# A hybrid S5 and differential-attention layer: the 1/rms chain of a head's outputs on GpSimd, the second map's factor as a tensor-scalar operation

## The chip, the cores and the metric

The kernel runs as one program on one core of a Trainium2 chip. The metric is the device time of one execution in microseconds (us); a kernel's time is the median of its runs. The engines are written as in the profile: PE (TensorE, with PEld for its weight loads), DVE (VectorE), ACT (ScalarE), POOL (GpSimd) and SP (SyncE, which here only issues DMAs).

## The reference, cut to what matters

The layer projects 1040 tokens (16 meta tokens and 1024 of input), runs an S5 mixer and a differential attention side by side, merges both by gates, and ends in a feed-forward stage. The change touches the attention, which has 8 heads with two softmax maps each:

```python
    s = jnp.einsum('bqhtd,bkhtd->bhtqk', qb, k, ...) * scale + bias[None, :, None]
    p = jax.nn.softmax(s, axis=-1)
    w = p[:, :, 0] - lam32 * p[:, :, 1]
    return jnp.einsum('bhqk,bkhe->bqhe', w.astype(v.dtype), v)
...
    xf = xf * lax.rsqrt(jnp.mean(xf * xf, axis=-1, keepdims=True) + EPS)   # _rmsnorm of a head's 128 outputs
...
    o = _rmsnorm(o, attn_subln[layer]) * (1.0 - lam_init)
    y_attn = o.reshape(bsz, L, ATTN_WIDTH) @ w_attn_out[layer]
```

## The kernel before

**Tiles and steps.** A head has 8 query tiles of 128 rows. Two tiles, a and b, make a pair, and the attention is a loop over 32 pairs, four steps to a head. What a step issues, and in which order, is written out by hand in a string (STEPS): each entry is an action and how many steps behind the newest pair it runs. The order of that string is the order in which each engine gets its instructions, since every engine works through its own instructions in order.

**What a step does.** PE makes the scores of a tile (L1163, L1164; six pieces, C10, C11, C12 for the second map and C00, C01, C02 for the first) into four PSUM buffers called S. DVE adds the bias, takes the minimum and writes the piece to the tile E0 or E1 (L1175, actions c10 to c02); each of E0 and E1 has two buffers, so a tile's E1 can be written only when POOL has read the E1 of two tiles earlier. ACT takes the exponential with its sum Z (L1181). DVE computes 1/Z and the second map's factor (L1187 and L1188, action coef; the factor is lambda times Z0/Z1). POOL scales E1 by the factor, adds E0 and E1 reversed into w, and copies 16 columns (L1195, L1197, L1198, action comb). PE transposes w (L1204, action T), ACT and DVE split the result into a high and a low part (L1214, L1218, actions hi and lo), and PE multiplies it with the values (L1239, action PV). Between these, PE does a gated linear unit of the S5 branch (L92 to L94, action GLU); its last product is one POOL instruction a step (L1374, action post2). POOL also splits a weight (L174) about once a head and scales a head's outputs (L1297, action mulq) twice a head.

**The chain.** ACT sums the squares of a tile's outputs (L1259). When a head's 8 tiles are done, the generator o_norm turns the 8 sums into 1/rms by an integer first guess and three Newton steps, on tiles of 128x8 (ss, ory, ora). It yields after each operation, and the actions n3a, n2b, n3b, n1a, n1b, n0a, n2a, n0b of a step each run it to its next yield. So a head's chain takes eight yields in one step and four in the next. These two of a head's four steps are called its chain steps below, and the other two its plain steps:

```python
STEPS = (... "sqb:4 ... mulq:1 ... n3a:3 ... combb:2 ... n2b:4 PV2y:3 post:2 exp0a:1 lo1a:2 n3b:4 n1a:2 n1b:1 post2:2 "
         "coefa:1 bcC:3 ... n0a:2 n2a:2 ... n0b:0 c00b:1 T1b:2 c01b:1 exp1b:1 hi1b:2 comba:1 GLUb:1 ")
for s_ in "ab":
    for n in range(4):
        FREE[f"n{n}{s_}"] = lambda: next(norm[0], None)
```

The result is read one step later by a transpose on PE (action bcT) and then, by way of DMAs, by L1297. Head 6 runs its chain in the string after the loop (TAIL, action n), and head 7 after that, when POOL has no work.

Of the kernel before, what the change touches and what calls it, by code (L numbers as in the profile page):

```python
# [11 lines left out]
I32 = mybir.dt.int32  # L12
AF = mybir.ActivationFunctionType
ALU = mybir.AluOpType
# [10 lines left out]
EPS = 1e-6  # L25
NT = S // 128
# [25 lines left out]
def tile_hybrid_encoder(ctx, tc, A, out, dbg=None, stop=None):  # L52
    nc = tc.nc
# [28 lines left out]
    V = nc.vector  # L82

    def mul(o, a, b):
        V.tensor_tensor(out=o, in0=a, in1=b, op=ALU.mult)
# [617 lines left out]
    nlam = cst.tile([128, 1], F32, tag="nlam", name="nlam")  # L703
# [114 lines left out]
    def warm(n):  # L818
        ps = pst([128, 512], "sm", "warm")
        for _ in range(n):  # L820
# [6 lines left out]
                           op1=ALU.add, accum_out=ms[:NM, 0:1])  # L827
# [302 lines left out]
    def ptl(pool, tag, shape, dt=F32, bufs=1):  # L1130
        return pool.tile(shape, dt, tag=tag, name=tag, bufs=bufs)
# [52 lines left out]
    def w_coef(i):  # L1184
        t = IT[i]
        rz = HT[i // NT]["rz"][:, i % NT]
        V.reciprocal(rz, t["Z"])  # L1187
        V.scalar_tensor_tensor(out=t["cf"][:, 0:1], in0=rz[:, 1:2], scalar=nlam, in1=t["Z"][:, 0:1],  # L1188
                               op0=ALU.mult, op1=ALU.mult)

    def w_comb(i):

# [65 lines left out]
        tp = PO["t", i // 2][:, i % 2]  # L1258
        nc.scalar.activation(tp, tp, AF.Square, scale=hd["rz"][:, qt, 0:1], accum_out=hd["ss"][:, qt:qt + 1])  # L1259

    def o_norm(h, a, b):

        hd = HT[h]
        ss, rz = hd["ss"][:, a:b], hd["rz"][:, a:b, 0]
        if a == 0:
            hd["y"] = ptl(osp, "ory", [128, NT], F32, 3)
        y, v = hd["y"][:, a:b], ptl(osp, "ora", [128, NT])[:, a:b]
        V.tensor_scalar(out=ss, in0=ss, scalar1=1.0 / 128, scalar2=EPS, op0=ALU.mult, op1=ALU.add)
        yield
        V.tensor_scalar(out=y.bitcast(I32), in0=ss.bitcast(I32), scalar1=-0.5, scalar2=float(0x5F3759DF),  # L1270
                        op0=ALU.mult, op1=ALU.add)
        yield
        for _ in range(3):
            mul(v, y, y)
            yield
            V.scalar_tensor_tensor(out=v, in0=v, scalar=-0.5, in1=ss, op0=ALU.mult, op1=ALU.mult)
            yield
            V.scalar_tensor_tensor(out=y, in0=v, scalar=1.5, in1=y, op0=ALU.add, op1=ALU.mult)
            yield
        mul(y, y, rz)  # L1280
        yield

    def o_bcT(h):
# [188 lines left out]
    norm = [iter(())]  # L1472
# [22 lines left out]
    for x in range(2):  # L1495
        s_ = "ab"[x]
        for m in range(2):
            ACTS[f"exp{m}{s_}"] = lambda p, m=m, x=x: ex_map(2 * p + x, m)
            for c in range(3):
                ACTS[f"C{m}{c}{s_}"] = lambda p, m=m, c=c, x=x: sc_mm(2 * p + x, m, c)  # L1500
                ACTS[f"c{m}{c}{s_}"] = lambda p, m=m, c=c, x=x: sc_tt(2 * p + x, m, c)
        for n, f in (("T", w_T), ("hi", w_hi), ("lo", w_lo)):
            for g in range(3):
                ACTS[f"{n}{g}{s_}"] = lambda p, f=f, g=g, x=x: f(2 * p + x, g)
        for n, f in (("coef", w_coef), ("comb", w_comb), ("sq", o_sq)):
            ACTS[n + s_] = lambda p, f=f, x=x: f(2 * p + x)
# [36 lines left out]
    def c_fill():  # L1543

        for us in (0,), (1,):
            for n in range(KD - 1):
                for c in range(2):
                    c_mm(us[0], c, 0, n, n + 1)
                    yield

    cf = c_fill()
# [4 lines left out]
    def run(steps):  # L1556
        for n in steps.split():
            n, _, p = n.partition("@")
            ACTS[n](int(p)) if p else FREE[n]()
# [12 lines left out]
    for j in range(3, NP + 1):  # L1572
# [8 lines left out]
        def at_(k, d):  # L1581

            h, q = divmod(j - d - k, 4)
            return h if q == 0 and 0 <= h < H else None

        h = at_(1, LC)
        if h is not None:
            load_head(h + 1)
        h = at_(3, LC)
        if h is not None:  # L1590
            load_q(h + 1, 1)
        h = at_(3, LP - 4)
        if h is not None:
            load_v(h + 1)
        h = at_(3, LS + 7)
        if h is not None and h < H - 3:
            o_st(h)
        h = at_(3, LS + 2)
# [4 lines left out]
        h = at_(3, LS)  # L1603
        if h is not None:
            norm[0] = o_norm(h, 0, NT)
    def tail_o():
# [3 lines left out]
        for a, n in ((0, 2), (2, 2), (4, 1)):  # L1610
# [4 lines left out]
                 "s0": lambda: o_split(0, 0, 2), "s1": lambda: o_split(0, 2, 2), "s2": lambda: o_split(0, 4, 1),  # L1615
                 "w0": lambda: w_next(U_A[0], 0), "w1": lambda: w_next(U_A[0], 1), "f": fill_c(1)})
    run(TAIL)
    norm[0] = o_norm(7, 0, NT)
    assert not (mulq or fill or wq or any(GQ))
    o_fa(6, 2)  # L1620
    o_fa(6, 3)
# [503 lines left out]
```

## Time and profile before

| | |
|---|---|
| median of 3 runs | 1904.03 us (1900.61 to 1904.47) |
| the profiled execution, its own time | 1903.11 us |
| its span, first to last instruction | 1900.9 us |
| PE busy | 1827.6 us (96%) |
| DVE busy | 1268.6 us (67%) |
| ACT, POOL busy | 867.9 us (46%), 871.6 us (46%) |
| mean granted TensorE clock | 0.989 |

The span is what the trace covers; 2.2 us of the execution's own time lie around it. The shares are means over the whole program. The loop over the pairs takes the time from about 690 to 1080 us, and there the busy shares are 95% for PE, 90% for DVE, 72% for ACT and 73% for POOL.

### The profile page before, as it was taken

Reading aid. Unit: us, or ns where it says so; the run is one execution under the profiler, and the core shown is the slowest. Engines: PE = TensorE matmul, PEld = TensorE weight load, DVE = VectorE, ACT = ScalarE, POOL = GpSimd, SP = SyncE. Lnnn points to the kernel's source line nnn. Section 1 sums busy time; section 2 is a strip of 40 time slices with the busy share of each in tenths; the row PEclk is TensorE's granted clock in tenths of the full one; section 3 lists DMA queues with packets and bytes.
Section 4 is the critical chain, followed back from the end, with each engine's and each line's share of the span. In section 5 each row is a group of like instructions: output and inputs, shape, how many; then the busy total and the mean of one; then the engine's idle time right before and its main releaser. Section 6 shows DMA issues by size and latency. Waiting matters only on the chain. (4 is left out here: it accounts for less than half of the span.)

```text
span 1900.9 us, 31037 instructions
## 1 busy us (share of the span) xinstructions
PE 1827.6 (96%) x11306; PEld 1642.2 (86%) x11306; DVE 1268.6 (67%) x2601; ACT 867.9 (46%) x1597; POOL 871.6 (46%) x803
## 2 busy tenths in 40 slices
PE   8998999899999989999999899999999999999999
PEld 7997888889999889999999888998788887888887
DVE  6699997763544688989999864369554545654543
ACT  4324343233433367777767632234555554433332
POOL 3068999643332177777767500005765652400000
PEclk8999999999999999999999999999999999999999
DMA  7423323337678565454554346431644448986563
GB/s 218 121 76 86 99 89 109 99 103 235 234 245 290 199 172 148 128 155 140 154 145 143 108 161 219 133 117 56 214 146 157 148 156 304 345 282 202 183 210 116
DMA packets 230535, 315.89 MB, mean 166 GB/s; under 512 B 39560, under 2 KB 140472, under 8 KB 230344
## 3 DMA queue, kind: packets, MB, share of 16 engines
q1 hardware_dynamic: 209952, 283.14, 47.1%
q10 hardware_dynamic: 20432, 30.78, 4.4%
q8 instruction: 89, 1.46, 0.3%
q14 instruction: 62, 0.51, 0.1%
HBM read 212.28 MB, written 99.48 MB: 164 GB/s over the span
## 5 line engine op out<-in xcount | busy, mean ns | idle before, releaser
L89 DVE TENSOR_TENSOR fp<-fr,fp 128x1024 fp32r<-128x1024 f32 x112 | 141.1, 1306 | 128.0 <-ACT fp L88 127.4
L92 PE MATMUL ps<-wh,hnh 128*128 128x256 f32 x768 | 221.3, 288 | 4.7 <-DVE qraw L969 3.5
L93 PE MATMUL ps<-wh,hnl 128*128 128x256 f32 x768 | 219.1, 285 | 4.6 <-DVE hnl L89 4.6
L94 PE MATMUL ps<-wl,hnh 128*128 128x256 f32 x768 | 218.8, 285 | 0.0
L88 ACT CAST fp<-fr 128x1024 fp32r<-128x1024 f32 x112 | 110.4, 1050 | 180.8 <-PE pf L94 159.2
L94 PE MATMUL pf<-fp 128*128 128x512 f32 x448 | 174.5, 390 | 1.3 <-DVE fp L89 1.3
L92 PE MATMUL pf<-fp 128*128 128x512 f32 x448 | 174.5, 390 | 0.5 <-ACT fp L88 0.4
L93 PE MATMUL pf<-fp 128*128 128x512 f32 x448 | 174.3, 389 | 0.0
L1181 ACT ACTIVATE E<-E,st 128x1040 f32<-128x1040 f32 x128 | 149.4, 1167 | 47.4 <-DVE st L1175 37.7
L1175 DVE CUSTOM_DVE_ANT_0 E<-S,Tb,st 128x344 f32<-128x344 f32 x256 | 146.7, 574 | 27.1 <-PE S L1164 5.7
L1197 POOL TENSOR_TENSOR w<-E,E 128x1040 f32<-128x1040 f32 x64 | 155.4, 2427 | 5.3
L92 PEld LDWEIGHTS ps<-wh,hnh 128*128 128x128 f32 x768 | 147.7, 192 | 6.9 <-DVE qraw L969 4.1
L93 PEld LDWEIGHTS ps<-wh,hnl 128*128 128x128 f32 x768 | 147.8, 192 | 4.9 <-DVE hnl L89 4.8
L94 PEld LDWEIGHTS ps<-wl,hnh 128*128 128x128 f32 x768 | 148.0, 193 | 0.0
L1163 PE MATMUL S<-K,Q 128*128 128x344 f32 (+1 forms) x384 | 134.5, 351 | 3.1 <-issue 3.0
L92 PE MATMUL ps<-hnh,wh 128*128 128x512 f32 (+2 forms) x352 | 133.6, 380 | 0.0
L93 PE MATMUL ps<-hnh,wl 128*128 128x512 f32 (+2 forms) x352 | 132.3, 376 | 1.3 <-POOL wl L174 1.0
L94 PE MATMUL ps<-hnl,wh 128*128 128x512 f32 (+2 forms) x352 | 131.4, 373 | 0.0
L89 DVE TENSOR_TENSOR swl<-w1r,swh 128x512 fp32r<-128x512 f32 x70 | 79.6, 1167 | 70.4 <-ACT swh L88 70.3
L1214 ACT CAST W<-wt 128x384 fp32r<-128x384 f32 x192 | 89.3, 481 | 79.3 <-PE wt L1204 71.6
L1164 PE MATMUL S<-K,Q 128*128 128x344 f32 (+1 forms) x384 | 123.5, 323 | 0.0
L1195 POOL TENSOR_SCALAR E<-E,st 128x1040 f32<-128x1040 f32 x64 | 74.4, 1163 | 97.1 <-DVE st L1188 55.3
(428 smaller groups left out, 5328.4 us busy)
## 6 DMA issues: line engine op xcount, KB each, us to landing
fr<-ad SPq DMA_DIRECT2D x56, 512.0 KB
ad<-r SPq DMA_DIRECT2D x91, 256.0 KB
raw<-in_w_in_dram SPq DMA_DIRECT2D x44, 512.0 KB
w<-in_w_ff_dram SPq DMA_DIRECT2D x32, 512.0 KB
wd<-w SPq DMA_DIRECT2D x32, 512.0 KB
Q<-qd SPq DMA_DIRECT2D x128, 128.0 KB
fr<-wd SPq DMA_DIRECT2D x32, 512.0 KB
w1r<-in_w_ff_dram SPq DMA_DIRECT2D x28, 512.0 KB
```

The source lines that it names most:

```text
L88: nc.scalar.copy(hi, src)
L89: (eng or nc.vector).tensor_tensor(out=lo, in0=src, in1=_f(hi), op=ALU.subtract)
L92: nc.tensor.matmul(o, l[0], r[0], start=start, stop=False, **kw)
L93: nc.tensor.matmul(o, l[1], r[0], start=False, stop=False, **kw)
L94: nc.tensor.matmul(o, l[0], r[1], start=False, stop=stop, **kw)
L1163: nc.tensor.matmul(ps[:, 0:n], qa[:, qs], k, start=True, stop=False)
L1164: nc.tensor.matmul(ps[:, 0:n], qb[:, qs], k, start=False, stop=True)
L1175: V.tensor_tensor_reduce(out=t["E", m][:, c0:c0 + n], in0=t.pop(("S", m, c))[:, 0:n], in1=HT[h]["Tb"][:, b0:b0 + n], scale=1.0, scalar=mn ...
L1181: nc.scalar.activation(t["E", m], t["E", m], AF.Exp, bias=t["mn"][:, m:m + 1], scale=-1.0, accum_out=t["Z"][:, m:m + 1])
L1195: nc.gpsimd.tensor_scalar(out=E1, in0=E1, scalar1=t["cf"][:, 0:1], scalar2=0.0, op0=ALU.mult, op1=ALU.add)
L1197: nc.gpsimd.tensor_tensor(out=w[:, 112:], in0=_rev(E0), in1=_rev(E1), op=ALU.add)
L1214: nc.scalar.copy(WT[p, g][:, :, 0, x], IT[i]["tp", g])
```

## The change

o_norm gets an engine and takes GpSimd where none is given, so the chains of heads 0 to 6 move from DVE to POOL. GpSimd gets no scalar_tensor_tensor here: the -0.5 becomes one extra operation ahead of the Newton steps, and the +1.5 one extra in each of the three. A chain of 12 instructions becomes one of 16. The number of yields stays at 12, so each operation stands at the same place in STEPS. Head 7 is given VectorE by name and runs the new 16 operations there. Beside this, w_coef computes the factor by a tensor_scalar with two per-row scalars, where it was a scalar_tensor_tensor.

```diff
-        V.scalar_tensor_tensor(out=t["cf"][:, 0:1], in0=rz[:, 1:2], scalar=nlam, in1=t["Z"][:, 0:1],
-                               op0=ALU.mult, op1=ALU.mult)
+        V.tensor_scalar(out=t["cf"][:, 0:1], in0=rz[:, 1:2], scalar1=nlam, scalar2=t["Z"][:, 0:1],
+                        op0=ALU.mult, op1=ALU.mult)
...
-    def o_norm(h, a, b):
+    def o_norm(h, a, b, eng=None):
+        G = eng or nc.gpsimd
...
-        V.tensor_scalar(out=ss, in0=ss, scalar1=1.0 / 128, scalar2=EPS, op0=ALU.mult, op1=ALU.add)
-        yield
-        V.tensor_scalar(out=y.bitcast(I32), in0=ss.bitcast(I32), scalar1=-0.5, scalar2=float(0x5F3759DF),
+        G.tensor_scalar(out=ss, in0=ss, scalar1=1.0 / 128, scalar2=EPS, op0=ALU.mult, op1=ALU.add)
+        yield
+        G.tensor_scalar(out=y.bitcast(I32), in0=ss.bitcast(I32), scalar1=-0.5, scalar2=float(0x5F3759DF),
                         op0=ALU.mult, op1=ALU.add)
+        G.tensor_scalar(out=ss, in0=ss, scalar1=-0.5, scalar2=None, op0=ALU.mult)
         yield
         for _ in range(3):
-            mul(v, y, y)
+            G.tensor_tensor(out=v, in0=y, in1=y, op=ALU.mult)
             yield
-            V.scalar_tensor_tensor(out=v, in0=v, scalar=-0.5, in1=ss, op0=ALU.mult, op1=ALU.mult)
+            G.tensor_tensor(out=v, in0=v, in1=ss, op=ALU.mult)
             yield
-            V.scalar_tensor_tensor(out=y, in0=v, scalar=1.5, in1=y, op0=ALU.add, op1=ALU.mult)
+            G.tensor_scalar(out=v, in0=v, scalar1=1.5, scalar2=None, op0=ALU.add)
+            G.tensor_tensor(out=y, in0=v, in1=y, op=ALU.mult)
             yield
-        mul(y, y, rz)
+        G.tensor_tensor(out=y, in0=y, in1=rz, op=ALU.mult)
         yield
...
-    norm[0] = o_norm(7, 0, NT)
+    norm[0] = o_norm(7, 0, NT, V)
```

On POOL, in the first chain step of head 0, the order before holds the comb of tile b, post2 and the comb of tile a, one behind the other (E is a map, w the combined tile, sg the gated product):

```order
L1195 TENSOR_SCALAR E_8466<-E_8466,st 128x1040
L1197 TENSOR_TENSOR w_7406<-E_8517,E_8466 128x1040
L1198 COPY w_7406<-w_7406 128x16
L1374 TENSOR_TENSOR sg<-ggt,sg 128x256
L1195 TENSOR_SCALAR E_8573<-E_8573,st 128x1040
L1197 TENSOR_TENSOR w_7405<-E_8594,E_8573 128x1040
```

The same place after the change, from the copy of tile b's comb on (ss, ory and ora are the chain's tiles):

```order
L1198 COPY w_7406<-w_7406 128x16
L1271 TENSOR_SCALAR ory<-ss 128x8
L1273 TENSOR_SCALAR ss<-ss 128x8
L1276 TENSOR_TENSOR ora<-ory 128x8
L1278 TENSOR_TENSOR ora<-ora,ss 128x8
L1280 TENSOR_SCALAR ora<-ora 128x8
L1281 TENSOR_TENSOR ory<-ora,ory 128x8
L1377 TENSOR_TENSOR sg<-ggt,sg 128x256
L1276 TENSOR_TENSOR ora<-ory 128x8
L1278 TENSOR_TENSOR ora<-ora,ss 128x8
L1280 TENSOR_SCALAR ora<-ora 128x8
L1281 TENSOR_TENSOR ory<-ora,ory 128x8
```

Ten instructions of the chain now stand between the comb of tile b and the comb of tile a: six ahead of post2 (L1377 now) and four behind it.

On DVE, at the same place, the order before holds the chain among the low parts, the scores and the factor:

```order
L1218 TENSOR_TENSOR W<-wt,W 128x3x128
L1270 TENSOR_SCALAR ory<-ss 128x8
L1368 SCALAR_TENSOR_TENSOR sg<-sg,f 128x256
L1218 TENSOR_TENSOR W<-wt,W 128x3x128
L85 TENSOR_TENSOR ora<-ory 128x8
L1276 SCALAR_TENSOR_TENSOR ora<-ora,ss 128x8
L1278 SCALAR_TENSOR_TENSOR ory<-ora,ory 128x8
L1187 RECIPROCAL rz<-st 128x2
L1188 SCALAR_TENSOR_TENSOR st<-rz,nlam,st 128x1
L1175 ISA E_8666,st<-S,Tb_7842 128x352
```

The same place after the change:

```order
L1218 TENSOR_TENSOR W<-wt,W 128x3x128
L1371 SCALAR_TENSOR_TENSOR sg<-sg,f 128x256
L1218 TENSOR_TENSOR W<-wt,W 128x3x128
L1187 RECIPROCAL rz<-st 128x2
L1188 TENSOR_SCALAR st<-rz,nlam,st 128x1
L1175 ISA E_8668,st<-S,Tb_7842 128x352
```

The chain's rows are gone from DVE, and the factor (L1188) is a tensor-scalar operation; the order of the rest is the same.

## Rows read from the trace of the kernel before

**Rows 1.** Waits of PE in the attention loop: total us, times, longest us

```profile
PE wt L1204 <- DVE W L1218: 13.6, 8, 2.1
PE ot L1253 <- DVE W L1218: 4.8, 7, 1.0
```

**Rows 2.** Chain-step pairs, heads 0 to 5: us, busy (count) PE PEld DVE ACT POOL

```profile
751.75:778.54 26.79, 25.04 (x195) 24.14 (x193) 24.99 (x82) 18.05 (x43) 16.55 (x14) 1.00 0.50 140
...
sum 167.41, PE 153.23 PEld 147.78 DVE 156.29 ACT 109.28 POOL 108.63; mean PE 25.54 PEld 24.63 DVE 26.05 ACT 18.21 POOL 18.10
```

**Rows 3.** The same for the six plain-step pairs that follow them

```profile
778.54:802.01 23.47, 23.47 (x187) 23.24 (x186) 20.47 (x70) 18.38 (x41) 18.99 (x16) 1.00 0.48 135
...
sum 140.74, PE 140.74 PEld 139.42 DVE 123.07 ACT 110.36 POOL 117.22; mean PE 23.46 PEld 23.24 DVE 20.51 ACT 18.39 POOL 19.54
```

**Rows 4.** Timeline in head 2's first chain step: start us, us, engine, line

```profile
861.45 2.41 POOL L1197 TENSOR_TENSOR w<-E,E 128x1040 f32<-128x1040 f32 x1
...
861.76 2.12 DVE L85 TENSOR_TENSOR ora<-ory 128x8 f32<-128x8 f32 x1
...
864.00 0.55 DVE L1218 TENSOR_TENSOR W<-wt,W 128x384 fp32r<-128x384 f32 x1
...
864.61 0.55 PE L1204 MATMUL wt<-idn,w 128*128 128x128 f32 x3 [1.47 <-DVE W L1218]
```

**Rows 5.** Instructions on tile ora, all heads: ns min/median/max, first and last start

```profile
L85 DVE TENSOR_TENSOR ora<-ory x24: 156/450/2311, 756.5 to 1097.8; 128x8 f32<-128x8 f32 x24
...
L1278 DVE SCALAR_TENSOR_TENSOR ory<-ora,ory x24: 150/168/931, 757.2 to 1098.2; 128x8 f32<-128x8 f32 x24
```

**Rows 6.** Line 1270, the chain's first guess, columns as above

```profile
L1270 DVE TENSOR_SCALAR ory<-ss x8: 172/766/785, 755.1 to 1095.8; 128x8 int32<-128x8 int32 x8
```

**Rows 7.** Line 1188, the factor, columns as above

```profile
L1188 DVE SCALAR_TENSOR_TENSOR st<-rz,nlam,st x64: 219/219/1100, 662.9 to 1073.9; 128x1 f32<-128x1 f32 x64
```

**Rows 8.** POOL's timeline in the S5 set-up, instructions of 128x8

```profile
283.73 1.19 POOL L356 TENSOR_TENSOR TC<-TC,e 128x8 f32<-128x8 f32 x1
284.88 0.20 POOL L357 TENSOR_TENSOR tt<-TS,e 128x8 f32<-128x8 f32 x1
285.16 0.21 POOL L358 TENSOR_TENSOR TC<-TC,tt 128x8 f32<-128x8 f32 x1
285.33 0.20 POOL L356 TENSOR_TENSOR TS<-TC,e 128x8 f32<-128x8 f32 x1
```

**Rows 9.** Groups by shape on POOL, dearest of 128x8: busy us, mean ns

```profile
L356 POOL TENSOR_TENSOR TS<-TC,e 128x8 f32<-128x8 f32 x7 | 3.6, 520 | 0.0
```

**Rows 10.** Line 1197, the comb's sum on POOL: ns min/median/max

```profile
L1197 POOL TENSOR_TENSOR w<-E,E x64: 2397/2428/2523, 667.4 to 1075.5; 128x1040 f32<-128x1040 f32 x64
```

**Rows 11.** Timeline of a plain step (head 1 to 2): POOL's comb, first users

```profile
846.38 0.74 POOL L1374 TENSOR_TENSOR sg<-ggt,sg 128x256 f32<-128x256 f32 x1
...
847.63 1.14 POOL L1195 TENSOR_SCALAR E<-E,st 128x1040 f32<-128x1040 f32 x1 [0.50 <-DVE st L1188]
...
848.85 2.44 POOL L1197 TENSOR_TENSOR w<-E,E 128x1040 f32<-128x1040 f32 x1
...
...
851.50 1.30 POOL L1297 TENSOR_TENSOR osb<-osb,fb 128x512 f32<-128x512 f32 x1
...
852.73 0.52 DVE L1175 CUSTOM_DVE_ANT_0 E<-S,Tb 128x352 f32<-128x352 f32 x1
...
854.18 0.41 PE L1163 MATMUL S<-K,Q 128*128 128x344 f32 x1
...
855.05 0.49 PE L1204 MATMUL wt<-idn,w 128*128 128x128 f32 x3
```

**Rows 12.** POOL's timeline around the start of head 1's first chain step

```profile
801.80 1.30 POOL L1297 TENSOR_TENSOR osb<-osb,fb 128x512 f32<-128x512 f32 x1
```

**Rows 13.** PE's timeline behind the loop, where head 6's chain runs

```profile
1070.42 0.55 PE L1204 MATMUL wt<-idn,w 128*128 128x128 f32 x3 [1.80 <-DVE W L1218]
...
1078.65 0.55 PE L1204 MATMUL wt<-idn,w 128*128 128x128 f32 x3 [1.03 <-DVE W L1218]
```

## The prediction

> **What bounds the kernel now.** I read the page first: PE is busy 96% of the span, so only work that PE waits for can move the time, and the first question is where PE waits. In the attention loop the list of waits gives it two that count, both for the low parts that DVE makes of the transposed w: 13.6 and 4.8 us [rows 1]. DVE, not PE, is late there. Next I cut the loop into pairs of steps at DVE's factor of a tile b and set the pairs with a chain beside those without. The plain pairs are PE's alone: PE is busy for all of the 140.74 us of six of them, 23.46 us each [rows 3]. The chain pairs take 167.41 us for six, PE is idle for 14.2 of these (167.41 - 153.23), and DVE is busy 156.29 us where the plain pairs have 123.07 [rows 2, 3]. So the chain costs PE time, though PE does almost none of it.
>
> The timeline shows how. In head 2 the chain's square of 128x8 on DVE begins at 861.76 and takes 2.12 us; POOL's sum of two 128x1040 tiles runs from 861.45 to 863.86, and the little DVE instruction ends with it, at 863.88. The low part behind it starts at 864.00, and PE has then stood 1.47 us [rows 4]. The same square takes 156 ns at its fastest and 2311 at its slowest, the chain's product 150 and 931 [rows 5]; the first guess has a median of 766 ns against 172 when POOL has nothing to do (the last of the eight, head 7's) [rows 6]. These DVE instructions wait for POOL's running one. The factor does too, at times: 219 ns as a rule, 1100 at most [rows 7].
>
> **What is removed.** Six heads (0 to 5) have chain pairs between plain pairs. The pairs can't be compared as they stand, because DVE's lateness shifts the cut: a chain pair holds 195 matmuls and a plain pair 187 [rows 2, 3]. A pair with the mean of 191 at the plain pairs' pace takes 23.46 x 191 / 187 = 23.96 us. Twelve such pairs take 287.5 us where they now take 167.41 + 140.74 = 308.15. So **20.6 us** is all that the loop can give back, 3.4 us a head. It fits the idle 14.2 us and the longer busy time of PE where it stops and starts again. Behind the loop, in head 6's chain, PE waits 1.80 and 1.03 us for low parts held the same way [rows 13]; I count **2.0** of these 2.8, since comb and outputs of the last tiles are short of other work to hide behind.
>
> **What is added on POOL.** Sixteen instructions of 128x8 a head. Unhindered ones take 0.20 us in the set-up, and one that reads its forerunner's result starts 0.28 us after it (284.88 to 285.16), one that doesn't 0.17 us (285.16 to 285.33) [rows 8]. Each of the chain needs the one before, so I take 0.28 each, 4.5 us a head. The trace has no chain of tensor-scalar operations of this size on POOL; the ends are 0.17, and 0.60 from the dearest group's mean of 520 ns with the 0.08 between [rows 9]. I stay near the low end because POOL's comb sum, 64 times in this loop, always takes between 2397 and 2523 ns [rows 10]: POOL isn't held there by DVE, and after the change DVE has still fewer instructions that could.
>
> POOL is busy 18.10 us of a chain pair and 19.54 of a plain one [rows 2, 3]. With 4.5 more it has 22.6 of some 24 us: nearly full, but with room to recover in the plain pair. What counts is who waits for it inside the chain step. One instruction stands ahead of comb b, where POOL waits for the factor anyhow. Ten stand between comb b and comb a, 2.8 us. In a plain step POOL goes from comb b's copy straight to post2 at 846.38, then stands 0.50 us and starts comb a at 847.63 [rows 11]; in a chain step comb a then starts 2.5 us later (2.8 with the small gaps, less the 0.5, and POOL's start behind the last small one), its sum ends at about 853.8 instead of 851.29. Two users follow. PE's transposes of that w begin at 855.05, 3.5 us after POOL is through with the comb (its next instruction starts at 851.50), so they stay covered. DVE writes the next E1 at 852.73, 1.4 us behind the sum that must have read the old one [rows 11]: **DVE now waits 1.1 us there**, with its factor and all later scores behind it. PE's matmul at 854.18 needs the S buffer that this DVE instruction frees at 853.25; its 0.93 us of slack [rows 11] leave 0.2 us of PE time.
>
> In heads 1, 3 and 5 it is worse: the scaling of outputs runs on POOL up to 803.10, 1.1 us into the step that begins at 802.01 [rows 12], where in the other heads the scaling is done before the step (it ends at 852.8, [rows 11]). There comb a is about 1.2 us later again, DVE waits 2.3 us, PE 1.3 or 1.4. The second chain step has five small instructions, four of them between the combs, 1.1 us, and starts late; its comb a delays DVE by 0.7 us, inside the 0.93. So POOL takes back 3 x 0.2 + 3 x 1.3 = **4.5 us**.
>
> **The factor.** A tensor-scalar operation with one tensor input: the nearest rows are 219 ns for the form before and 172 for a tensor-scalar of 128x8 [rows 6, 7]; at most 0.05 us x 64 = 3 us of DVE time, hidden, since DVE has 3 us a plain pair to spare (23.46 - 20.51). Whether it still waits for POOL no row shows: the first guess, a tensor-scalar too, does at 128x8 [rows 6]. From below it is free, from above it keeps the 0.9 us of its slowest (1100 - 219) in heads 1, 3 and 5, again inside PE's 0.93. I count nothing. Head 7's chain gains four instructions on DVE of 0.17 us each: 0.7 us, behind PE's matmuls of the output projection: nothing.
>
> **The sum.** 20.6 + 2.0 - 4.5 = 18.1 us off the profiled execution's 1903.1: 1885.0. Its own time lies 0.9 us under the median of the runs; so I predict **1886.0**.
>
> **A rule against the change.** By the rows, 156 to 172 ns on DVE where nothing holds it [rows 5, 6] become 0.28 us on POOL [rows 8]. The Trainium skill, GPSIMD Engine Reference, section Engine selection, advises VectorE for elementwise work, with GpSimd about twice as slow for two inputs. The trace agrees on that price (0.28 against 0.17). By the rule the kernel would pay the longer chain, which gives the 1921 of the first rival; by the rows DVE's chain costs what it waits, not what it works, which gives the sum above.
>
> **Rivals.**
> *The longer chain is what is paid* (slower). If PE's stops came from the chain's own length and not from being held by POOL, 16 x 0.28 = 4.5 us would replace 12 x 0.17 = 2.0 [rows 6, 8]: 2.5 us a head, 17 us for seven, 1921. It decides if PE's waits in chain steps don't fall. Against it: the square that ends with POOL's sum [rows 4]. Chance 0.04.
> *POOL's small instructions are held* (slower). One row of the set-up takes 1.19 us for 128x8 [rows 8]. At that price ten take 11.9 us, comb a comes over 11 us late, PE loses some 10 us a head in place of 3.4: 6 x 6.6 = 40 more, 1944. It turns the sign from about 0.6 us an instruction on, where POOL takes back what DVE gives (comb a 5.6 us late, PE 3.3 and 4.5 us, 23 us in all). Chance 0.03.
> *POOL takes back more* (faster still). At 0.40 us each comb a is 3.6 us late, DVE waits 2.2 and 3.4, PE 1.3 and 2.5 us: 11.4 us, so 1893; from 1890 to 1899 in all. For it: POOL's 22.6 of 24 us. Chance 0.17.
> *No change*, 1904 within 4: another hand-over, such as the exponentials behind DVE, holds the chain steps at their length. Against it: ACT is busy 18.21 us of a chain pair and the plain pairs run without any wait of PE. Chance 0.08.
> *As worked out*, 1880 to 1890: 0.68.
>
> **Range and chances.** The low end is the case in which POOL takes nothing back and both stops behind the loop go, 20.6 + 2.8: 1880.6, with the uncertainty of the runs 1878. The high end takes in most of the third rival: 1896. A measurement of this kernel can tell about 0.2%, 3.8 us, from no change. Faster by more than that: 0.68 + 0.17, and a little of the "no change" case, 0.87; within it 0.06; slower 0.07.
>
> **What the new profile would show.** Right: PE's wait for low parts falls from 18.4 us in the loop to under 5, the chain pairs come to about 24.2 (even heads) and 25.3 us (odd), small POOL instructions stand 0.28 us apart, and DVE's first E1 instruction behind a chain step waits for POOL's sum, 1 to 2.3 us. Wrong: small POOL instructions of 0.5 us and more, PE waiting for w itself (then the 3.5 us of cover was wrong), or a comb of tile b that starts late in plain steps, which would mean that POOL doesn't recover between chains.

## The result and the profile after

| | before | after |
|---|---|---|
| median on one chip | 1902.32 us (1898.63 to 1904.47, 4 runs) | 1884.43 us (1883.56 to 1887.48, 4 runs) |
| ratio to before | | 0.9898, interval 0.9881 to 0.9914 |
| profiled execution, its own time | 1903.11 us | 1887.48 us |
| its span | 1900.9 us | 1885.3 us |
| DVE busy | 1268.6 us | 1234.1 us |
| POOL busy | 871.6 us | 890.0 us |
| twelve pairs of heads 0 to 5 | 308.15 us | 290.73 us |

The kernel is 17.9 us faster (1902.32 - 1884.43), and the interval of the ratio leaves room from 16 to 23; 18.1 was forecast. The last line of the table is the loop of the prediction: the before value is the sum of [rows 2, 3], the after value is worked out below.

The waits of PE in the attention loop, of the kernel after, from 690 to 1065 us (columns as in [rows 1]):

```profile
PE S L1163 <- DVE st L1175: 2.8, 4, 0.8
PE wt L1204 <- DVE W L1218: 0.9, 1, 0.9
PE ot L1253 <- DVE W L1218: 0.9, 2, 0.7
```

The same two rows of the kernel before, in the same stretch ([rows 1] reach to 1080 us and take in two stops more behind the pairs):

```profile
PE wt L1204 <- DVE W L1218: 10.8, 6, 2.1
PE ot L1253 <- DVE W L1218: 4.2, 6, 1.0
```

These two waits have shrunk to 0.9 us each, and none of what is left of them lies in the twelve pairs: the one at L1204 comes behind them (below), the two at L1253 come ahead of the first chain, as in the kernel before. What is left in the heads' chain steps is a new wait for a score buffer (S) that DVE frees: 2.5 of the 2.8 us, in heads 1, 3 and 5.

Pairs of steps of the kernel after, first the chain-step pairs, then the plain-step pairs (columns as in [rows 2]; the cut is DVE's reciprocal just ahead of the factor):

```profile
754.39:778.40 24.01, 24.01 (x191) 23.80 (x190) 20.59 (x71) 17.89 (x41) 19.46 (x29) 1.00 0.52 146
802.34:827.35 25.01, 24.16 (x191) 23.77 (x190) 20.57 (x71) 17.88 (x41) 22.16 (x33) 1.00 0.57 157
...
sum 147.26, PE 144.78 PEld 143.06 DVE 123.54 ACT 107.64 POOL 127.27; mean PE 24.13 PEld 23.84 DVE 20.59 ACT 17.94 POOL 21.21
...
sum 143.47, PE 143.47 PEld 142.25 DVE 123.04 ACT 112.30 POOL 116.92; mean PE 23.91 PEld 23.71 DVE 20.51 ACT 18.72 POOL 19.49
```

147.26 + 143.47 = 290.73, so the loop gave back 308.15 - 290.73 = 17.4 us. Of these 11.7 are idle time of PE (14.2 before, 147.26 - 144.78 = 2.5 after); for the rest PE is busy for less time. DVE is as busy in a chain pair (20.59) as in a plain one (20.51); before it was 26.05 [rows 2]. The first row is head 0: PE is busy for all of its 24.01 us. The second is head 1: 0.85 us of 25.01 are idle. All heads with an even number look like the first (23.97 to 24.01), all with an odd one like the second (25.01, 25.02, 25.26).

Where the 0.85 us come from shows in the timeline of head 1's first chain step, of the kernel after:

```profile
812.59 2.41 POOL L1197 TENSOR_TENSOR w<-E,E 128x1040 f32<-128x1040 f32 x1
...
815.04 0.53 DVE L1175 CUSTOM_DVE_ANT_0 E<-S,Tb 128x352 f32<-128x352 f32 x1 [1.85 <-POOL w L1197]
...
815.62 0.42 PE L1163 MATMUL S<-K,Q 128*128 128x344 f32 x1 [0.85 <-DVE st L1175]
```

POOL's sum ends at 815.00; DVE, which has waited for 1.85 us, writes the E1 buffer that the sum has read; PE gets its S buffer when DVE is through. It is the chain of hand-overs that the prediction named. In the even heads DVE waits too, but PE doesn't (head 2, of the kernel after):

```profile
862.94 0.53 DVE L1175 CUSTOM_DVE_ANT_0 E<-S,Tb 128x352 f32<-128x352 f32 x1 [0.75 <-POOL w L1197]
```

The list of DVE's waits in the loop has six of these, one a head, of 0.7 to 1.9 us:

```profile
DVE E L1175 <- POOL w L1197: 7.8, 6, 1.9
```

POOL's timeline between comb b and comb a in head 0's first chain step, of the kernel after:

```profile
758.76 0.20 POOL L1198 COPY w<-w 128x16 f32<-128x16 f32 x1
759.04 0.20 POOL L1271 TENSOR_SCALAR ory<-ss 128x8 int32<-128x8 int32 x1
759.33 0.26 POOL L1273 TENSOR_SCALAR ss<-ss 128x8 f32<-128x8 f32 x1
759.55 0.20 POOL L1276 TENSOR_TENSOR ora<-ory 128x8 f32<-128x8 f32 x1
759.84 0.20 POOL L1278 TENSOR_TENSOR ora<-ora,ss 128x8 f32<-128x8 f32 x1
760.13 0.24 POOL L1280 TENSOR_SCALAR ora<-ora 128x8 f32<-128x8 f32 x1
760.45 0.20 POOL L1281 TENSOR_TENSOR ory<-ora,ory 128x8 f32<-128x8 f32 x1
760.61 0.74 POOL L1377 TENSOR_TENSOR sg<-ggt,sg 128x256 f32<-128x256 f32 x1
761.32 0.19 POOL L1276 TENSOR_TENSOR ora<-ory 128x8 f32<-128x8 f32 x1
...
762.38 1.13 POOL L1195 TENSOR_SCALAR E<-E,st 128x1040 f32<-128x1040 f32 x1
```

The small instructions last 0.19 to 0.26 us and start 0.22 to 0.32 us apart. Six take 1.57 us (759.04 to 760.61), the four behind post2 1.06 (761.32 to 762.38): 2.63 us where 2.8 was worked out.

The factor, of the kernel after (columns as in [rows 7]):

```profile
L1188 DVE TENSOR_SCALAR st<-rz,nlam,st x64: 272/273/276, 664.9 to 1056.6; 128x1 f32<-128x1 f32 x64
```

It got longer, 273 ns against 219, and its slowest takes 276 where the slowest before took 1100 [rows 7].

Behind the twelve pairs, where head 6's chain runs (eight of its yields still in the loop's last step, four in TAIL), two short stops of PE are left in the kernel after:

```profile
1063.76 0.55 PE L1204 MATMUL wt<-idn,w 128*128 128x128 f32 x3 [0.94 <-DVE W L1218]
1066.42 0.55 PE L1204 MATMUL wt<-idn,w 128*128 128x128 f32 x3 [0.72 <-DVE W L1218]
```

Together 1.66 us. The kernel before has the 1.80 and 1.03 of [rows 13] there, 0.57 us at L1253 between them, and one more, which the prediction did not count:

```profile
1082.77 0.55 PE L1204 MATMUL wt<-idn,w 128*128 128x128 f32 x3 [1.22 <-DVE W L1218]
```

That is 4.6 us in all. How much came back shows at PE's last product with a chain's result (first and last start; before, then after):

```profile
L1307 PE MATMUL yb<-idn,ory x16: 270/272/323, 1086.3 to 1103.4; 128*128 128x128 f32 x16
L1310 PE MATMUL yb<-idn,ory x16: 270/272/324, 1068.2 to 1085.6; 128*128 128x128 f32 x16
```

The last of the twelve pairs ends at 1059.71 before and at 1045.12 after, by the same cut. From there to this product the kernel before takes 43.7 us, the kernel after 40.5: 3.2 us came back by then. At the end of the span only 1.0 is left (1900.9 - 1059.71 against 1885.3 - 1045.12). About 1.6 of the 3.2 are lost in a later stage, where the clock is lower. The same work of the kernel before, then of the kernel after (columns as in [rows 2]):

```profile
1333.00:1343.00 10.00, 9.26 (x41) 7.65 (x42) 5.55 (x6) 4.94 (x10) 7.53 (x6) 1.00 0.85 303
1315.00:1325.00 10.00, 8.97 (x32) 7.25 (x33) 5.34 (x6) 4.38 (x8) 7.54 (x6) 0.83 0.88 318
```

In the second the mean granted clock is 0.83, and eight matmuls take up to 0.63 us each where they took 0.39. The same spell stands at this place in the trace of every run below with the sixteen operations, and in none with the twelve; what brings it about is not shown.

The parts and the span: 17.4 in the twelve pairs and 1.0 behind them make 18.4, while the spans differ by 15.6 (1900.9 - 1885.3). The rest is ahead of the chains: in this execution the first chain pair begins at 754.39, before at 751.56, 2.8 us later. The program up to there differs only in the factor's form, and 2.0 of the 2.8 stand already at the first factor (664.9 against 662.9 [rows 7]). In the repeated run of the kernel after (below) the first chain pair begins at 750.04. So the difference of the medians, 17.9, is the better measure, and the parts agree with it.

### The profile page after: what moved, and what is told of

It reads as the page before. It is cut to its first block, busy times and chain, and to the rows that moved or that the text cites. A ratio compares the mean times of both kernels' runs of the same rounds, so it can differ in the third digit from the quotient of the medians.

```text
span 1885.3 us, 31070 instructions
## 1 busy us (share of the span) xinstructions
PE 1826.4 (97%) x11306; PEld 1643.5 (87%) x11306; DVE 1234.1 (65%) x2521; ACT 868.5 (46%) x1597; POOL 890.0 (47%) x915
## 5 line engine op out<-in xcount | busy, mean ns | idle before, releaser
L1239 PE MATMUL o<-W,VV 128*128 128x256 f32 x768 | 115.1, 286 | 0.0
```

Source lines behind the costliest of these rows:

```text
L1239: nc.tensor.matmul(PO[p], v, w, start=g == 0 and n == 0, stop=g == 2 and n == 8)
```

## The experiments

The kernels were run beside the kernel before on the same chip, and each ratio is to that. "Twelve pairs" is the sum over heads 0 to 5, cut as above.

| kernel | median us | ratio to before (interval) | twelve pairs us |
|---|---|---|---|
| before | 1902.32 to 1906.1 | 1 | 308.15 |
| after | 1884.43 | 0.9898 (0.9881 to 0.9914) | 290.73 |
| chain alone | 1884.27 | 0.9895 (0.988 to 0.991) | 290.42 |
| factor alone | 1905.49 | 1.0007 (0.9998 to 1.0015) | 308.98 |
| old chain on DVE, moved | 1890.5 | 0.9925 (0.9912 to 0.9937) | 294.59 |
| new chain on DVE | 1913.62 | 1.0054 (1.0041 to 1.0067) | 316.05 |
| ten and four more on POOL | 1912.59 | 1.0039 (1.0027 to 1.005) | 314.06 |
| chain on POOL, spread | 1880.99 | 0.9883 (0.9869 to 0.9896) | 287.40 |
| after, again | 1884.14 | 0.9901 (0.9887 to 0.9915) | 290.76 |
| spread, again | 1879.71 | 0.9876 (0.9861 to 0.9891) | 287.39 |

The theory: DVE's small instructions cost by being held behind POOL's running one, so the engine that they run on matters, and on POOL they cost only what POOL is late for others. The first rival: it is the number of instructions or their length that is paid. The second: the factor's new form brings part of the gain.

**The chain alone.** The kernel after with the factor as it was.

```diff
-        V.tensor_scalar(out=t["cf"][:, 0:1], in0=rz[:, 1:2], scalar1=nlam, scalar2=t["Z"][:, 0:1],
-                        op0=ALU.mult, op1=ALU.mult)
+        V.scalar_tensor_tensor(out=t["cf"][:, 0:1], in0=rz[:, 1:2], scalar=nlam, in1=t["Z"][:, 0:1],
+                               op0=ALU.mult, op1=ALU.mult)
```

> The changed kernel with the factor as it was, a scalar_tensor_tensor. Theory (DVE's chain instructions were held by POOL's running one, and the chain's move is the whole gain): 1884 us, within 2 us of the changed kernel; the factor, 219 ns as a rule and held up to about 1 us in heads 1, 3 and 5, is hidden behind PE. Rival (the new form of the factor brings a part of the gain): 1888 us or more.

Measured: 1884.27 us (1882.49 to 1886.25, 4 runs), ratio 0.9895, as the whole change. The old factor is still held at times in this run, up to 1123 ns:

```profile
L1188 DVE SCALAR_TENSOR_TENSOR st<-rz,nlam,st x64: 218/219/1123, 664.6 to 1055.1; 128x1 f32<-128x1 f32 x64
```

It costs PE nothing: the twelve pairs take 290.42 us, with the new factor 290.73. The gain is the chain's move.

**The factor alone.** The kernel before with the new factor (the diff above the other way round).

> The kernel before with the factor alone as a tensor-scalar operation, the chain on DVE as it was. Theory: 1900 to 1903 us; the factor takes 0.27 us in place of 0.22 and is not held any more, which takes at most 0.9 us off DVE in each of three chain steps. Rival (the factor matters): 1898 us or less.

Measured: 1905.49 us (11 runs), ratio 1.0007 with an interval that holds 1. The factor takes 273 ns in it too, at most 276; the chain's square on DVE is held as before, up to 2365 ns. The time is 2.5 us above the expected range, so the small gain that was expected is not there. The factor's part of the change is worth nothing that can be told, in either direction.

**The old chain on DVE, moved.** The kernel before, its twelve operations a head unchanged and still on DVE, but six of a step's actions together, right ahead of the factor of tile b. There POOL mostly stands waiting for that factor. A head's chain now takes six yields in each of two steps, and TAIL gets one more n, since only six yields of head 6 run ahead of it. (The kernel's string has n0a:1, not the n0a:2 of the cut ahead of the prediction; the number has no effect on these actions.)

```diff
-    ... "T2b:3 coefb:2 C01a:1 " ... "T1a:2 n3a:3 hi0a:2" ... "bcT:3 n2b:4 " ... "n3b:4 n1a:2 n1b:1 post2:2" ...
+    ... "T2b:3 n3a:3 n2b:4 n3b:4 n1a:2 n1b:1 n0a:1 coefb:2 C01a:1 " ... "T1a:2 hi0a:2" ... "bcT:3 " ... "post2:2" ...
```

> The kernel before with its twelve instructions on DVE, but six of them stand together right ahead of the factor of tile b, in two steps a head, where POOL mostly has nothing to do but wait for that factor. The chain's work on DVE stays the same. Theory (DVE loses what it is held, not what it works): the chain's instructions take 0.15 to 0.2 us each, POOL's comb b starts about 1 us later inside its slack, and the kernel comes to 1884 to 1890 us; in heads 1, 3 and 5 one of them can still be held by the scaling of outputs, up to 1.3 us. Rival (the chain's length on DVE is what costs): 1900 to 1904 us, no change.

Measured: 1890.5 us (1886.01 to 1891.58, 5 runs), ratio 0.9925, half a microsecond above the expected range. The chain's operations on DVE in this kernel (columns as in [rows 5]):

```profile
L85 DVE TENSOR_TENSOR ora<-ory x24: 151/167/169, 753.6 to 1085.6; 128x8 f32<-128x8 f32 x24
L1276 DVE SCALAR_TENSOR_TENSOR ora<-ora,ss x24: 160/166/2310, 753.8 to 1085.8; 128x8 f32<-128x8 f32 x24
L1278 DVE SCALAR_TENSOR_TENSOR ory<-ora,ory x24: 158/166/172, 754.0 to 1086.0; 128x8 f32<-128x8 f32 x24
```

The square has fallen from 156/450/2311 to 151/167/169 (the one row of 2310 is behind the loop, in head 6's chain). DVE does the same work with the same number of instructions, and some 13 us are won by where they stand (1903.75 - 1890.5 beside the kernel before; 308.15 - 294.59 = 13.6 in the twelve pairs). So the hold was the cost, not the work. At the old place too the hold is what PE waits for: unheld, the square of [rows 4] would take 0.16 us, 1.96 less than its 2.12, and PE stood 1.47 us there.

What stays is in part a hold again. In heads 1, 3 and 5 the first of the six (L1268) falls under POOL's scaling of the outputs, here in head 1:

```profile
801.66 1.30 POOL L1297 TENSOR_TENSOR osb<-osb,fb 128x512 f32<-128x512 f32 x1
801.70 1.29 DVE L1268 TENSOR_SCALAR ss<-ss 128x8 f32<-128x8 f32 x1
```

In the other heads L1268 takes 0.17 us. In these three PE waits for S, 0.77 us each. They are 2.3 of the 7.2 us by which the twelve pairs are longer than those of the spread version below; where the others go was not traced.

**The new chain on DVE.** The kernel after, with DVE where GpSimd stands: sixteen operations a head instead of twelve, in the places of before.

```diff
-        G = eng or nc.gpsimd
+        G = eng or nc.vector
```

> The changed kernel with its sixteen operations a head on DVE instead of POOL (factor as changed). Theory (DVE's small instructions wait for POOL's running one): the four more a head add 0.17 us each where nothing holds them and about 0.6 us where a tensor-scalar is held like the first guess (766 against 172 ns), so 0.7 to 2.5 us a head for six heads on a path that already makes PE wait: 1908 to 1920, PE's waits for low parts above 18.4 us. Rival (the rewritten operations, not the engine, bring the gain): at or under 1895.

Measured: 1913.62 us (1909.87 to 1916.63, 5 runs), ratio 1.0054: slower than before, by the engine alone 29.5 us over the kernel after (1884.14 in the run beside it). PE's waits for low parts in this kernel, from 690 to 1065 us:

```profile
PE wt L1204 <- DVE W L1218: 12.3, 6, 2.1
PE ot L1253 <- DVE W L1218: 5.9, 10, 1.2
```

That is 18.2 us, where the kernel before has 10.8 + 4.2 = 15.0 in this stretch: 3.2 more, so the waits rose, as had been expected. In the stretch of [rows 1], taken up to the same work, they are 21.2 against 18.4. The other part of the twelve pairs' 7.9 us (316.05 - 308.15) is that PE is busy longer, and some of that is clock. Its chain pairs (columns as in [rows 2]) show it:

```profile
805.01:834.29 29.28, 25.61 (x195) 23.99 (x194) 27.34 (x87) 18.05 (x43) 19.05 (x17) 1.00 0.50 147
857.73:888.09 30.36, 27.72 (x195) 26.73 (x194) 28.21 (x89) 18.42 (x43) 17.78 (x15) 0.89 0.42 122
```

With the same 195 matmuls PE is busy 25.61 us in head 1 and 27.72 in head 2, where the mean granted clock is 0.89.

**Ten and four more on POOL.** The kernel after with fourteen more squares of 128x8 a head on POOL, ten between comb b and comb a of the first chain step and four in the second. They add work whose result is not used.

```diff
         G.tensor_scalar(out=ss, in0=ss, scalar1=-0.5, scalar2=None, op0=ALU.mult)
+        for _ in range(0 if eng else 2):
+            G.tensor_tensor(out=v, in0=y, in1=y, op=ALU.mult)
...
             G.tensor_tensor(out=y, in0=v, in1=y, op=ALU.mult)
+            for _ in range(0 if eng else 4):
+                G.tensor_tensor(out=v, in0=y, in1=y, op=ALU.mult)
```

> The changed kernel with ten more small POOL instructions (the square repeated, result unused) between comb b and comb a of the first chain step, and four more in the second: 14 more of 0.28 us a head. Theory (past the 1.4 us of cover of E1 and the 0.93 us of the S buffers each microsecond on POOL is one on PE): comb a comes 2.8 us later, DVE waits about 3.5 us (other heads) and 4.6 us (heads 1, 3, 5), PE 2.6 and 3.6 us; with the second step's four 16 to 22 us more than the changed kernel, 1900 to 1906 us, all of the gain. Rival (POOL is idle for a quarter of the loop, so it takes the work without a loss): 1884 to 1887 us.

Measured: 1912.59 us (1910.15 to 1915.21, 8 runs), ratio 1.0039. By the ratios that is (1.0039 - 0.9898) x 1904 = 27 us over the kernel after, more than the 16 to 22 expected, and 6.6 above the expected range of times; it ends slower than before. PE's wait for S in the loop:

```profile
PE S L1163 <- DVE st L1175: 18.4, 7, 3.6
```

The stops are 2.5 us in the even heads and 3.58 in the odd ones, where 2.6 and 3.6 had been worked out. In the odd heads, where DVE's and PE's slack is used up already, ten more small instructions cost 3.58 - 0.85 = 2.73 us, 0.27 each: they pass their time from start to start on to PE. That makes 18.2 us (3 x 2.5 + 3 x 3.58), 15.7 over the kernel after. The twelve pairs are 314.06 - 290.73 = 23.3 us longer; the other 7.6 are that PE is busy longer. Four of the six chain pairs have a mean clock of 0.94, as the first and not the second of these rows:

```profile
752.29:780.44 28.15, 25.65 (x190) 25.26 (x189) 20.62 (x73) 17.71 (x41) 22.15 (x43) 0.94 0.45 126
...
909.93:938.82 28.89, 25.24 (x197) 24.61 (x196) 20.63 (x71) 18.98 (x45) 24.96 (x47) 1.00 0.45 130
```

A matmul takes 25.65 / 190 = 0.135 us of busy time in the first and 25.24 / 197 = 0.128 in the second, so 1.3 us a pair, 5 us in all. And in head 6's chain behind the pairs PE waits for w itself:

```profile
1081.30 0.69 PE L1204 MATMUL wt<-idn,w 128*128 128x128 f32 x2 [2.51 <-POOL w L1198]
```

23.3 + 2.5 are 25.8 of the 27, which is as near as the intervals of the two ratios allow.

**The chain on POOL, spread.** The kernel after, with the same sixteen operations on POOL, but in a step three actions behind post2 and three behind comb a, so that four small instructions and not ten stand between comb b and comb a. TAIL gets one more n here too.

```diff
-    ... "T1a:2 n3a:3 hi0a:2" ... "bcT:3 n2b:4 " ... "lo1a:2 n3b:4 n1a:2 n1b:1 post2:2 coefa:1" ... "n0a:1 n2a:2 " ... "n0b:0 " ... "comba:1 GLUb:1 "
+    ... "T1a:2 hi0a:2" ... "bcT:3 " ... "lo1a:2 post2:2 n3a:3 n2b:4 n3b:4 coefa:1" ... "comba:1 n1a:2 n1b:1 n0a:1 GLUb:1 "
```

> The changed kernel with POOL's chain spread out: three actions between post2 and comb a and three behind comb a, six to a step, in place of eight between comb b and the end. Theory (POOL gives back through the buffer of E1, which DVE can't write before comb a has read it): DVE's waits for POOL of 0.75 and 1.8 us and PE's of 0.8 us in heads 1, 3 and 5 shrink to under 0.3, and the kernel is 2 to 3 us faster than the changed one, about 1882 us. Rival (only the amount of POOL's work counts, not its place): 1884 us as the changed kernel.

Measured: 1880.99 us (1879.52 to 1885.23, 4 runs), ratio 0.9883. The chain pairs of this kernel (columns as in [rows 2]):

```profile
752.40:776.30 23.90, 23.90 (x190) 23.74 (x189) 20.53 (x71) 17.73 (x41) 19.64 (x30) 1.00 0.54 161
800.27:824.16 23.89, 23.89 (x190) 23.74 (x189) 20.54 (x73) 17.70 (x41) 22.19 (x33) 1.00 0.60 176
...
sum 143.35, PE 143.35 PEld 142.41 DVE 123.09 ACT 106.29 POOL 127.91; mean PE 23.89 PEld 23.74 DVE 20.52 ACT 17.71 POOL 21.32
```

PE is busy throughout in all six, in odd heads too. With the plain pairs (144.05) the twelve take 287.40 us: the prediction's floor for the loop was 287.5. The median is 3.4 us under that of the kernel after, but the runs of the two overlap, so both were run again on one chip.

> The changed kernel again, beside the next one on the same chip: 1884 to 1886.

> The version with the chain's POOL operations moved to where POOL has nothing late behind them, again, beside the changed kernel. Theory (POOL takes back the three stops of PE in heads 1, 3 and 5, 2.5 us, and the late starts of DVE): 2 to 4 us under the changed kernel's time of this call, ratio to it 0.998 to 0.999. Rival (the earlier 1880.99 was the spread of the runs): within 1 us of it.

Measured: the kernel after 1884.14 us (1882.35 to 1887.48, 4 runs), the spread version 1879.71 (1878.81 to 1880.56, 4 runs): 4.4 us less, a little over the 2 to 4 expected, and the two sets of runs don't overlap. 3.4 of these are in the twelve pairs (290.76 - 287.39). This is the fastest version tried.

## Why the prediction was right

**What the loop can give back** was right. The signs came as named: PE's waits for low parts fell from 18.4 us to 2.6 in the stretch of [rows 1] (under 5 forecast), and the chain pairs take 24.0 us in even heads and 25.1 in odd ones (24.2 and 25.3 forecast). 20.6 us were worked out (308.15 - 287.5), and the spread version, in which nothing is taken back, shows 308.15 - 287.40 = 20.75. The changed kernel's loop gave back 17.4.

**What POOL takes back** was right in mechanism and too large. Predicted were 0.2 us of PE in even heads and 1.3 in odd ones, 4.5 in all; measured were nothing and 0.83 (2.5 in all), and 290.73 - 287.40 = 3.3 us of loop time. The step that was off is how late comb a comes. DVE waits 0.75 us in even heads and 1.85 in odd ones in place of 1.1 and 2.3; with the 1.4 us of slack of a plain step that makes POOL late by 2.2 and 3.3 us, not 2.5 and 3.7. A part of it is the ten instructions (2.63 us and not 2.8); why the scaling of outputs costs 1.1 and not 1.2 stays open. PE's slack of 0.93 us [rows 11] was right: 1.85 - 0.93 = 0.92 against the 0.85 seen, and 0.75 is inside it.

**Behind the loop** the size was wrong. 2.0 us were taken from two stops of 2.83. PE stopped there for 4.6 us, and 3.2 came back by the end of the attention; of these 1.0 is left at the end of the span, since 1.6 went to a lower clock in a later stage, of which the prediction has nothing, and 0.5 elsewhere.

**The sum** is nearer than its terms, and that is luck. POOL took back 1.2 us less than forecast (3.3 and not 4.5), and 1.0 us less came back behind the loop (1.0 and not 2.0); the two errors cancel. 20.75 - 3.3 + 1.0 = 18.4 by the traces, 17.9 by the medians and 18.1 in the forecast are one number, given an interval from 16 to 23.

**The price on POOL** held: 0.19 to 0.26 us an instruction, 0.22 to 0.32 from start to start, against the 0.28 taken. POOL is busy 21.21 us of a chain pair in place of 22.6, mostly since the busy time leaves out the gaps between small instructions (16 of 0.21 us are 3.4 and not 4.5). The prediction's 0.28 against 0.17, in its rule against the change, sets a time from start to start on POOL beside a duration on DVE: by durations the square takes 0.20 us on POOL and 0.17 on DVE in the kernel after (L1276, heads 0 to 6 and head 7), so the trace shows a factor of 1.2 at this size and not of two. No small one in the six heads is held as the row of 1.19 us was [rows 8]; a single one, behind them, took 1.15, and what held it is shown in the last section.

**The factor** was put at 0.17 to 0.22 us and at a gain of at most 3 us of DVE time. It takes 0.273, so it costs DVE 54 ns x 64 = 3.5 us. The sign was wrong, the bound on its size nearly right, and that it is hidden was right: both runs that change it alone show no difference. What was left open, whether it still waits for POOL, is settled: of 64 none takes over 276 ns, in the kernel before's order too.

**The rivals.** That the longer chain is paid falls with the two kernels on DVE: the old chain moved is 1890.5 with DVE's work unchanged, and the new chain on DVE is slower than before where the same operations on POOL are faster. That POOL's small instructions are held falls with their durations. That POOL takes back more falls with 2.5 us of stops, and that nothing changes with 17.9 us. The margin on POOL is thin, though: with ten more small instructions in the gap and four behind it the change is a loss.

## What to carry to other kernels

Before moving small instructions, look at the slowest of a group beside the fastest: 156 against 2311 ns for one form says that they wait and don't work, and then either another engine or another place in the order takes the wait away. On the engine that they go to, ask what stands behind them: the same sixteen operations cost 3.4 us less in the loop when they run behind the hand-over instead of ahead of it. A slack that is worked out from one step's timeline (here 0.93 us) is worth writing down, since past it each further small instruction on POOL was 0.27 us of a stop of PE.

## What the runs showed of the hardware

**Which small instructions of DVE are held.** While POOL runs its sum of two 128x1040 tiles, DVE's square (tensor-tensor) and its first guess (tensor-scalar) of 128x8 wait, 2311 and 785 ns at most [rows 5, 6]. Under POOL's scaling of outputs a scalar-tensor-tensor of 128x8 waits, 931 at most [rows 5], and the old factor of 128x1: it starts at 802.01, takes 1.10 us and ends at 803.11 [rows 7], the scaling at 803.10 [rows 12]. The factor as a tensor-scalar with two per-row scalars doesn't wait (276). The Trainium skill, SBUF — State Buffer, section Who interferes with whom, says that a DVE instruction with two SBUF inputs, or in a mode that uses two ports, and a GpSimd instruction that reads SBUF exclude each other for the whole instruction, and that a DVE instruction with one SBUF input outside these modes is free. The trace agrees for the first kind: the square ends at 863.88, POOL's sum at 863.86 [rows 4]. The first guess has one tensor input and is held; it would be of the second kind, but no run here shows its mode. The free factor fits if its scalars don't count as inputs; no run here tests that by itself.

**POOL is held in the same way when DVE starts first.** In head 6's chain of the kernel after:

```profile
1061.96 1.27 DVE L1425 SCALAR_TENSOR_TENSOR oT<-oT,sub,oT 128x1024 fp32r<-128x1024 f32 x1
1062.14 1.15 POOL L1281 TENSOR_TENSOR ory<-ora,ory 128x8 f32<-128x8 f32 x1
```

DVE's instruction ends at 1063.23, POOL's product, 0.20 us elsewhere, at 1063.29. The row of 1.19 us in [rows 8] is of this kind too: DVE's L174 runs there from 283.36 to 284.85, and POOL's product ends at 284.92. So the chain is safe on POOL where no long instruction of DVE that holds it runs beside it.

**A stop of PE can cost more than its length.** The kernel before has 0.94 of the clock in a chain pair where PE stops for 2.1 us (columns as in [rows 2]):

```profile
801.81:830.26 28.45, 26.34 (x194) 25.55 (x193) 26.65 (x83) 18.38 (x43) 19.05 (x17) 0.94 0.51 150
```

Read as the lower level, 1.2 in place of 2.4 GHz, that is an estimated 28.45 x 0.06 x 2 = 3.4 us at half clock, and PE is busy 26.34 us there where head 0 has 25.04 [rows 2]. It is so in heads 1 and 3 of that run and not in head 5, which stops as long. With more on POOL, stops of 2.5 and 3.6 us were followed by it in heads 0, 1, 2 and 5 and not in 3 and 4. With the new chain on DVE it follows stops of 2.0 us in heads 0, 2 and 4 and not those of 2.1 us in heads 1, 3 and 5, so the length of the stop alone doesn't decide it. The same shows in the later stage above: PE stops for 2.0 us ahead of it in the kernel before too, and its clock stays at 1.00 there. The stops of 0.8 us of the kernel after never were followed by it: its twelve pairs all have 1.00. So some of the time that the change gives back is clock, not idle time.
